# The encoder's tail in 512-token matmuls on groups of 1024 tokens, with the embeddings' product moved into the last attention units

## The chip, the cores and the metric

The kernel runs on 1 core of one Trainium2 chip. The metric is the device time of one execution in microseconds (us); the time before is the median of three runs. The engines are called by the names of the profile: PE is TensorE, DVE VectorE, ACT ScalarE, POOL GpSimd, and SP the engine whose queue issues the transfers (DMA).

## The reference

One encoder layer for two requests (prompt and sample) of 2048 tokens each, width 1024, all in float32. Two attention branches (a window of 128 tokens to both sides, and a neighbourhood on a grid of 64 columns) give 1024 columns of output per token; then come an output projection, a gate and an embeddings' product:

```python
x = x + jnp.concatenate([o_a, o_b], axis=-1) @ w_out
gate = jax.nn.sigmoid(x @ w_ple_gate)
return x + (p @ w_ple) * gate          # p: 256 columns per token
```

These three lines are the tail, and the change lies in them.

## The kernel before

**Precision.** Matmuls take two operands in a shortened float32. Each operand is split into a high part (a cast, on ACT) and the rest (a subtraction, mostly on DVE), and each product is three matmuls: high x high and the two mixed ones.

**Attention.** Blocks of 128 tokens are projected (`proj_a`, `proj_b`) and attended to in units (`unit_a`, `unit_b`). TensorE's order is written out by hand. A stream of "filler" matmuls (L943) is drawn from while a unit runs: each filler matmul has a price (108 for 256 tokens, 215 for 512), each unit has a budget of filler (L953: 10320 for most units of the second branch, `TAIL` for the last six, when no projection is left), and the tables PLAN_A and PLAN_B say at which part of the budget a step of the attention is put in. Weight splits wait as jobs in a list and are put in by `pump` and `flush`. The attention's outputs go to DRAM, those of the second branch in an order of their own (by columns of the grid).

**The tail.** Everything is transposed: rows are columns of the layer, and the moving operand of a matmul is a tile of tokens. `TW` is 256 here, so there are 16 tiles of tokens.

- `out_ahead` (L866) computes the output projection of one tile in the plain way: 8 row blocks x 8 x 3 matmuls of 256 tokens, the residual added by DVE (L882), the result x1 stored to DRAM. Three tiles (`AHEAD - 1`) are filler of the last six attention units, a fourth stands behind them. `load_o`, `split_o` and `load_ev` bring and split what it needs.
- All other products of the output projection and of the gate are made by seven products instead of eight (a scheme of Strassen's kind): the weight is cut into four blocks of 512 x 512, two tiles of 256 tokens with the two halves of the columns make four operand blocks, and sums of weight blocks (made ahead, in DRAM, `sums`) meet sums of operand blocks. A group is 512 tokens: six groups for the output projection (stage 0), eight for the gate (stage 1), seven steps each, 48 matmuls of 256 tokens a step (`product`, L1074).
- `prep` (L1039) makes the operand of a step two steps ahead: the sum in a tile of its own (POOL and DVE), the cast (ACT, L1068), the subtraction (DVE or POOL, L1053), each over 1024 elements a row.
- `result` (L1103) takes a product out of PSUM. In stage 0 the residual is added and x1 stored. In stage 1 a result is finished by an addition (L1124), tanh on ACT (L1128), a multiplication with the embeddings' product, which stands in PSUM (L1129), and the addition of x1 out of the operand's tile (L1131), then stored to the output (L1134).
- The embeddings' product (`ple_of`, L1150) is computed in stage 1, six matmuls of 256 tokens a block, between the products.

In the tail, DVE, ACT, POOL and SP are partly ordered by a scheduler, partly as written: what is wrapped in `P` or `pin` is kept in the order of the program.

Of the kernel before, what the change touches and what calls it, by code (L numbers as in the profile page):

```python
# [69 lines left out]
SB = 5  # L70
# [8 lines left out]
TAIL = 9300  # L79
HOLD = {"wa": 20, "wb": 12, "wp": 0}  # L80
TW = 256
NU = SEQ // TW
AHEAD = 4
# [15 lines left out]
def emit(ctx, tc, io):  # L99
# [706 lines left out]
    o_st, o_rs = {}, {}  # L806

    def fproj(ps, w, m, xs, nk, mm_):
        for k in range(nk):
            if mm_ is mm:  # L810
                flush(f"o{k // 4}")
                flush(("wa", "wb")[m // 4] + str(KT - 1))
            for i, (a, b) in enumerate(((0, 0), (1, 0), (0, 1))):
                mm_(ps, w[m // 4][k][:, a, 128 * (m % 4):128 * (m % 4) + 128], xs(k, b),
                    start=(k == 0 and i == 0), stop=(k == nk - 1 and i == 2))
                yield 108

    def load_o(n, tail):
        if n < len(tiles):
            s, u = tiles[n]  # L820
            o_st[n] = []
            for i in range(2):
                st = main.tile([128, 2, TW], F32, tag="stage", name="oa", bufs=2)
                nc.sync.dma_start(st, oa_d[s].rearrange("(i j p) t -> i p j t", p=128, j=2)[i, :, :, TW * u:TW * u + TW])
                o_st[n].append(st)
            for i in range(2):
                if tail:
                    st = ap.tile([128, 2, 4, 64], F32, tag="sq", name="ob", bufs=2)
                else:
                    st = main.tile([128, 2, 4, 64], F32, tag="s", name="ob", bufs=SB)  # L830
                nc.sync.dma_start(st.rearrange("p j c t -> p (j c) t"),
                                  ob_d[s][u // 2].rearrange("p (i j) c t -> i p (j c) t", i=2)
                                  [i, :, :, 64 * (u % 2):64 * (u % 2) + 64])
                o_st[n].append(st)

    def split_o(n, i):

        t = main.tile([128, 2, 2, 2, TW], F32R, tag="xr", name="o_r", bufs=2)
        st = o_st[n][2 * i:2 * i + 2]

        def job(dst, src):
            nc.scalar.copy(dst[0], src)
            nc.vector.tensor_tensor(out=dst[1], in0=src, in1=dst[0].bitcast(F32), op=ALU.subtract)
        for j in range(2):
            if i == 0:
                jobs.append((f"o{i}", partial(job, [t[:, j, a] for a in range(2)], st[j])))
            else:
                for k in range(2):
                    jobs.append((f"o{i}", partial(job, [t[:, j, a, k].rearrange("p (r k c) -> p k r c", k=4, c=16)
                                                        for a in range(2)],  # L850
                                                  st[j][:, k].rearrange("p k (r c) -> p k r c", c=16))))
        o_rs.setdefault(n, []).append(t)

    def o_hi_lo(n):
        return lambda k, b: o_rs[n][k // 4][:, k % 4 // 2, b, k % 2, :]

    def load_ev(n, mp):

        if n < AHEAD - 1:
            ev = ap.tile([128, 2, TW], F32, tag="ev", name="ev", bufs=2)  # L860
        else:
            ev = main.tile([128, 2, TW], F32, tag="s", name="ev", bufs=SB)
        nc.sync.dma_start(ev, io["x_r"][n][:, 2 * mp:2 * mp + 2])
        return ev

    def out_ahead(n, evs=None):  # L866

        tail = n < AHEAD - 1
        if n > 0:
            split_o(n, 0)  # L870
            split_o(n, 1)
        if n != AHEAD - 2:
            load_o(n + 1, tail)
        for mp in range(4):
            ps = ptile([128, 2, TW], "pj", "pout")
            for kk in range(2):
                for i, c in enumerate(fproj(ps[:, kk, :], w_b[2], 2 * mp + kk, o_hi_lo(n), KT, mm)):
                    if tail and i % 5 == 4:
                        pump()
                    yield c  # L880
            ev = evs[mp] if evs else load_ev(n, mp)
            P(nc.vector.tensor_tensor(out=ev, in0=ps, in1=ev, op=ALU.add))  # L882
            nc.sync.dma_start(x1_d[n][:, 2 * mp:2 * mp + 2], ev)
# [41 lines left out]
    def paired(f, n):  # L925

        a, b = filler(f), filler(f + 1)
        half, w = (f - 2 * NT) // (2 * NT) + 1, []
        src, c0 = (w_in_c, 1024 * half) if half < 2 else (w_out_c, 0)
        yield from islice(a, n)  # L930
        yield from islice(b, n)
        w.append(load_w(main, "wa", src, c0, KT, half < 2))
        yield from a
        if half == 2:
            load_o(0, True)
            split_o(0, 0)
        yield from b
        if half == 2:
            split_o(0, 1)
        w.append(load_w(main, "wb", src, c0 + 512, KT, half < 2))  # L940
# [38 lines left out]
    with tc.tile_pool(name="c", bufs=1) as op:  # L979

        STEPS = ("a11", "a12", "s2", "s1", "s3", "a22", "s4")
        SLOT = {"s2": 0, "s3": 1, "s4": 2, "s1": 3}

        def load_q(i, name):

            out = []
            for j in range(4):
# [5 lines left out]
                tag = {"a11": f"wa{j}", "a12": f"wa{4 + j}", "s4": f"wb{j}", "a22": f"wb{4 + j}"}.get(name, f"{name}{j}")  # L993
# [3 lines left out]
                nc.sync.dma_start(raw, src)  # L997
                jobs.append((f"{i}{name}", partial(split_w, w, raw, None, tc.keep_in_program_order)))
                out.append(w)
            return out  # L1000

        ws = [{}, {}]
        w_p = []

        raws, opds = {}, {}
        groups = [(0, g) for g in range(AHEAD // 2, NU)] + [(1, g) for g in range(NU)]

        def raw_tile(name):
            return op.tile([128, 8, TW], F32, tag="raw", name=name, bufs=4)

        def load_raw(n):
# [4 lines left out]
            if stage == 0:  # L1016
                s, b = divmod(g, 4)
                oa, ob = raw_tile("oar"), raw_tile("obr")
                oav = oa.rearrange("p a t -> p (a t)").rearrange("p (k t) -> p k t", k=4)
                obv = ob.rearrange("p a t -> p (a t)").rearrange("p (k c t) -> p k c t", k=4, c=4)  # L1020
                nc.sync.dma_start(oav, oa_d[s].rearrange("(k p) t -> p k t", p=128)[:, :, 512 * b:512 * b + 512])
                nc.sync.dma_start(ob.rearrange("p a t -> p (a t)"), ob_d[s][b].rearrange("p j c t -> p (j c t)"))
                raws[n] = [oav[:, :, :TW], oav[:, :, TW:]] + [
                    [obv[:, k].rearrange("p c (r x) -> p r c x", x=16)[:, 4 * h:4 * h + 4] for k in range(4)] for h in range(2)]
            else:
                t = [raw_tile("x1r") for _ in range(2)]
                for h in range(2):
# [75 lines left out]
        def result(n, q, mp, ps, part):  # L1103
# [16 lines left out]
            if part == 0:  # L1120
                return
# [161 lines left out]
```

## Time and profile before

| | us |
|---|---|
| runs, median (lowest, highest) of 3 | 2585.34 (2582.66, 2585.56) |
| span of the profiled execution | 2584.1 |
| PE busy in it | 2531.9 (98%) |
| DVE busy | 1922.3 (74%) |
| ACT busy | 1392.3 (54%) |
| POOL busy | 792.2 (31%) |

The profiled execution's own time is its span; it lies inside the range of the runs. How to read the rows: in rows of groups, a row names the line, the engine, the operation, what it writes and reads, the shapes and the count, then the busy time and the mean length of one in ns, then the idle time of the engine just before and what ended it. In rows of the order of time come the start, the length and how many instructions were merged; a bracket gives the idle time before and what ended it. A matmul's length is longer than its spacing, since matmuls overlap: the spacing is read from starts. The granted clock is the share of full speed that TensorE was given.

### The profile page before, as it was taken

The numbers are of one execution on the slowest core, as the hardware profiler recorded it, in microseconds if no ns is written. First come the engines' busy times: TensorE is split into PE (matmuls) and PEld (weight loads), VectorE is DVE, ScalarE is ACT, GpSimd is POOL, SyncE is SP. The second block draws the span as 40 slices with busy tenths as digits, with TensorE's granted clock in tenths as the row PEclk, the third lists the DMA queues.
The fourth block names the chain that finished last, engine by engine and source line by source line (L and its number), as shares of the span: only waits on it lengthen the run. The fifth ranks groups of instructions, "written<-read, shape, count | busy, mean of one in ns | idle before, by whom it ended". The sixth has DMA issues, their size and how long they took to land.

```text
span 2584.1 us, 47172 instructions
## 1 busy us (share of the span) xinstructions
PE 2531.9 (98%) x16080; PEld 2268.0 (88%) x16080; DVE 1922.3 (74%) x5704; ACT 1392.3 (54%) x3327; POOL 792.2 (31%) x995
## 2 busy tenths in 40 slices
PE   8999999999989999999899999999999999999999
PEld 7888888888877888888788888887999999999999
DVE  7888888888886877887878777878665648555454
ACT  6666666666664666666666666666432214223222
POOL 3333323333223333333233333321132324233321
PEclk9999999999999999999999999999999999999999
DMA  6323342111243565555665555557584455232221
GB/s 203 107 90 109 107 102 81 55 60 58 60 119 123 171 196 150 183 184 170 211 187 155 184 173 154 155 153 216 167 280 167 153 172 182 85 121 85 79 82 46
DMA packets 227551, 357.51 MB, mean 138 GB/s; under 512 B 37968, under 2 KB 115408, under 8 KB 222160
## 3 DMA queue, kind: packets, MB, share of 16 engines
q1 hardware_dynamic: 227312, 354.51, 43.8%
q8 instruction: 128, 2.10, 0.3%
q14 instruction: 111, 0.91, 0.1%
HBM read 266.33 MB, written 105.92 MB: 144 GB/s over the span
## 4 chain that ended last, share of the span: by engine, by line
PE 85%; DVE 8%; ACT 3%; issue 2%; DMA 2%; POOL 1%; SPq 0%; DVEq 0%; ACTq 0%; POOLq 0%
PE pqk L212 12%; PE pvg L212 12%; PE acca L1087 11%; PE accc L1087 8%; PE pq L212 6%; PE pg L212 6%; PE pple L212 4%; PE pout L212 3%; PE ptb L215 3%; PE pk L212 3%; PE scb L212 3%; PE pob L212 3%; PE sc L212 3%; PE po L212 3%; PE pt L215 3%
## 5 line engine op out<-in xcount | busy, mean ns | idle before, releaser
L243 ACT ACTIVATE s<-s,nm 128x384 f32<-128x384 f32 (+4 forms) x512 | 307.2, 601 | 360.3 <-DVE nm L238 232.3
L212 PE MATMUL pvg<-wb,xr 128*128 128x512 f32 x1536 | 460.4, 407 | 0.0
L212 PE MATMUL pqk<-wa,xr 128*128 128x512 f32 x1536 | 444.0, 411 | 0.0
L308 POOL TENSOR_TENSOR xr<-stx,xr 128x512 fp32r<-128x512 f32 x190 | 245.1, 1298 | 186.7 <-ACT xr L307 179.4
L212 PEld LDWEIGHTS pqk<-wa,xr 128*128 128x128 f32 x1536 | 267.4, 190 | 37.7
L212 PEld LDWEIGHTS pvg<-wb,xr 128*128 128x128 f32 x1536 | 267.2, 189 | 31.1
L212 PE MATMUL pg<-wb,xr 128*128 128x512 f32 x768 | 232.6, 410 | 0.0
L212 PE MATMUL pq<-wa,xr 128*128 128x512 f32 x768 | 221.2, 402 | 2.8 <-DVE wa L160 2.8
L798 POOL TENSOR_TENSOR o_tb<-otb 128x256 f32<-128x256 f32 x64 | 48.9, 763 | 559.4 <-DVE otb L791 469.8
L1087 PE MATMUL acca<-opd,s 128*128 128x256 f32 x1344 | 164.7, 283 | 3.6 <-ACT r L1119 2.5
L1087 PEld LDWEIGHTS acca<-opd,s 128*128 128x128 f32 x1344 | 162.6, 192 | 4.4 <-ACT r L1119 2.7
L212 PEld LDWEIGHTS pq<-wa,xr 128*128 128x128 f32 x768 | 140.1, 190 | 26.4 <-DVE wa L160 3.8
L227 DVE CUSTOM_DVE_ANT_0 s<-scb,bias 128x288 f32<-128x288 f32 (+3 forms) x256 | 141.5, 553 | 21.0 <-PE scb L212 18.5
L212 PEld LDWEIGHTS pg<-wb,xr 128*128 128x128 f32 x768 | 138.0, 190 | 20.5
L212 PEld LDWEIGHTS pob<-p_t,vw 128*128 128x128 f32 (+2 forms) x832 | 131.7, 190 | 24.9 <-DVE q L719 3.7
L646 DVE SCALAR_TENSOR_TENSOR ks_b<-pktb,wk,ks_b 64x128 fp32r<-64x128 f32 x256 | 115.1, 450 | 44.1 <-ACT ks_b L645 33.8
L1053 POOL TENSOR_TENSOR opd<-sum,opd 128x1024 fp32r<-128x1024 f32 x28 | 69.8, 2494 | 233.6 <-ACT opd L1068 233.6
L645 ACT ACTIVATE ks_b<-pktb,wk 64x128 fp32r<-64x128 f32 x256 | 124.6, 487 | 30.7 <-DVE ks_b L646 24.5
L772 DVE TENSOR_TENSOR p_t<-ptb,p_t 128x368 fp32r<-128x368 f32 (+5 forms) x256 | 125.2, 490 | 18.4 <-ACT p_t L771 11.1
L215 PE MATMUL ptb<-rowwise,s 128*128 128x128 f32 (+2 forms) x832 | 133.4, 274 | 3.7 <-ACT s L243 3.7
L605 DVE TENSOR_TENSOR pr<-pt,pr 128x512 fp32r<-128x512 f32 x184 | 125.3, 684 | 14.9 <-ACT pr L604 13.9
L227 DVE CUSTOM_DVE_ANT_0 s<-sc,mask 128x384 f32<-128x384 f32 (+1 forms) x256 | 132.6, 537 | 3.1 <-PE sc L212 0.7
(201 smaller groups left out, 5846.2 us busy)
## 6 DMA issues: line engine op xcount, KB each, us to landing
stx<-x_b SPq DMA_DIRECT2D x128, 256.0 KB
vw<-v_d SPq DMA_DIRECT2D x112, 256.0 KB
stx<-x_a SPq DMA_DIRECT2D x64, 256.0 KB
stn<-x_n SPq DMA_DIRECT2D x64, 256.0 KB
v_d<-vb SPq DMA_DIRECT2D x64, 256.0 KB
x1r<-x_d SPq DMA_DIRECT2D x16, 1024.0 KB
y_t<-r SPq DMA_DIRECT2D x64, 256.0 KB
v_d<-vb SPq DMA_DIRECT2D x96, 128.0 KB
```

What stands on the lines that cost most here:

```text
L212: pinned(nc.tensor.matmul(out, lhsT, rhs, start=start, stop=stop))
L215: pinned(nc.tensor.transpose(out, in_, eye))
L227: nc.vector.tensor_tensor_reduce(out=s[:, :n], in0=ps[:, :n], in1=bias, scale=1.0, scalar=-3.0e38, op0=ALU.add, op1=ALU.max, accum_out=sm[ ...
L243: ex = nc.scalar.activation(ss[i][:, :n], ss[i][:, :n], AF.Exp, bias=nm[:, i:i + 1], accum_out=den[:, i:i + 1])
L308: low.tensor_tensor(out=lo, in0=raw, in1=hi.bitcast(F32), op=ALU.subtract)
L605: nc.vector.tensor_tensor(out=pr[:, 1], in0=pf, in1=pr[:, 0].bitcast(F32), op=ALU.subtract)
L645: nc.scalar.activation(hi, pkt[a:a + 64, i], AF.Copy, scale=wk[a:a + 64, 1:2])
L646: nc.vector.scalar_tensor_tensor(out=lo, in0=pkt[a:a + 64, i], scalar=wk[a:a + 64, 1:2], in1=hi.bitcast(F32), op0=ALU.mult, op1=ALU.subtract)
L772: nc.vector.tensor_tensor(out=lo, in0=pf, in1=hi.bitcast(F32), op=ALU.subtract)
L798: nc.gpsimd.tensor_tensor(out=o_t, in0=got["ot"][:, :, 0], in1=got["ot"][:, :, 1], op=ALU.add)
L1053: each(lambda x, y, z: pin(eng.tensor_tensor(out=x, in0=y, in1=z, op=ALU.subtract)), out, a, b)
L1087: pinned(nc.tensor.matmul(ps[:, kk], w[k][:, a, c:c + 128], o[:, b, k], start=i in (0, 1, 4) and kk == 0 and k == 0 and j == 0, stop=k == ...
```

## The change

`TW` becomes 512, so there are 8 tiles of tokens, and a group of the split products is 1024 tokens: four groups for the output projection and four for the gate, 7 steps of 48 matmuls of 512 tokens each. No tile is projected in the plain way any more.

The embeddings' product is computed ahead for all tiles (`ple_ahead`): tiles 0 to 4 (`AHEAD` is 5) are the filler of the last six attention units, whose budget falls from 9300 to 8600; tiles 5 to 7 stand behind them. ACT copies each block out of PSUM, and it is stored to DRAM (`ple_d`). In the gate it is loaded again block by block, and so is x1 for the residual (`load_x`: eight tiles in flight, two loads for each result).

Sums of operand blocks are formed in place in the loaded tiles (`combos`, on POOL and once on DVE), one step or more ahead; five operand tiles of 8 KB a row are in use. A step's operand is split in four pieces (`piece`) during the step before it. A result is one block of 128 rows x 512 tokens. The accumulators keep the four blocks of one chain in four banks of PSUM. All of this is wrapped in `P`, so that DVE, ACT, POOL and SP work in the order of the program. The weights of the first steps are loaded and split during the embeddings' product (`load_early`).

```diff
-TAIL = 9300
+TAIL = 8600
-TW = 256
+TW = 512
-AHEAD = 4
+AHEAD = 5
...
+    def split_p(n, later=False):
+        t = p_rs[n] = main.tile([128, 2, 2, TW], F32R, tag="xr", name="p_r", bufs=2)
+        def job(hi, lo, src):
+            nc.scalar.copy(hi, src)
+            nc.vector.tensor_tensor(out=lo, in0=src, in1=hi.bitcast(F32), op=ALU.subtract)
...
+    def ple_ahead(n, tail=False):
+        load_p(n + 1)
+        for m in range(KT):
+            ps = ptile([128, TW], "pj", "pple")
+            if m == 5 and n + 1 < len(tiles):
+                split_p(n + 1)
+            flush("p")
+            flush("p0")
+            for k in range(2):
+                w, c = early["p"][2 * (m // 4) + k], 128 * (m % 4)
+                for i, (a, b) in enumerate(((0, 0), (0, 1), (1, 0))):
+                    mm(ps, w[:, a, c:c + 128], p_rs[n][:, k, b], k == 0 and i == 0, k == 1 and i == 2)
+                    yield 215
+            if n > 0 or m > 5:
+                pump()
+            if tail:
+                ev = main.tile([128, TW], F32, tag="s", name="ev", bufs=SB)
             else:
+                ev = ap.tile([128, TW], F32, tag="ev", name="ev", bufs=2)
+            P(nc.scalar.copy(ev, ps))
+            nc.sync.dma_start(ple_d[n][:, m], ev)
...
-                   *(out_ahead(n) for n in range(AHEAD - 1)))
+                   *(ple_ahead(n) for n in range(AHEAD)))
...
-    with tc.tile_pool(name="c", bufs=1) as op:
+    with tc.tile_pool(name="c", bufs=1, reuse_waits="tile") as op:
...
+        def combos(n, i, k):
+            if i == 0:
+                if k == 0:
+                    raws[n, 4] = op.tile([128, 4, TW], F32, tag="raw", name="raw", bufs=5), False
+                less(nc.vector, n, k, 0, 2, 0)
+                less(nc.gpsimd, n, k, 4, 3, 0)
+            elif i == 2:
+                less(nc.gpsimd, n, k, 2, 3, 2)
+            elif i == 3:
+                less(nc.gpsimd, n, k, 4, 1, 4)
...
+        def piece(m, k):
...
+            P(nc.scalar.copy(hi, v))
+            P(nc.vector.tensor_tensor(out=lo, in0=v, in1=hi.bitcast(F32), op=ALU.subtract))
...
+        def product(m, mi):
...
+            for k in range(4):
+                o = opds[m, k]
+                for j, (a, b) in enumerate(((0, 0), (1, 0), (0, 1))):
+                    pinned(nc.tensor.matmul(ps, w[k][:, a, c:c + 128], o[:, b], start=i in (0, 1, 4) and k == 0 and j == 0,
+                                            stop=k == 3 and j == 2, skip_group_check=True))
...
         def load_x():
             if to_load:
+                x = main.tile([128, TW], F32, tag="stage", name="xres", bufs=2) if count[0] % 8 < 2 else \
+                    op.tile([128, TW], F32, tag="xres", name="xres", bufs=6)
+                P(nc.sync.dma_start(x, to_load.pop(0)))
...
+            P(nc.scalar.activation(r, ps if first else r, AF.Tanh, scale=0.5))
+            P(V.scalar_tensor_tensor(out=r, in0=r, scalar=1.0, in1=loaded.pop(0), op0=ALU.add, op1=ALU.mult))
+            P(V.scalar_tensor_tensor(out=r, in0=r, scalar=0.5, in1=loaded.pop(0), op0=ALU.mult, op1=ALU.add))
             load_x()
+            load_x()
...
+        load_raw(0, 0)
+        drain(ple_ahead(AHEAD, True))
+        load_raw(0, 1)
+        drain(ple_ahead(AHEAD + 1, True))
...
         for m in range(7 * len(groups)):
             n, i = divmod(m, 7)
+            if i >= 3:
+                load_raw(n + 1, i - 3)
...
+            for mi in range(4):
+                combos(n, i, mi)
+                for k in range(2 * mi, 2 * mi + 2) if mi < 2 else ():
+                    piece(m + 1, k)
+                result(n, i, mi, product(m, mi))
```

More of the change, by code (lines that the diff above doesn't have):

```diff
@@ L818, in load_o, with load_p @@
-    def load_o(n, tail):
+    ple_d = [dram.tile([128, KT, TW], F32, tag=f"ple_d{n}", name=f"ple_d{n}") for n in range(len(tiles))]
+    p_st, p_rs, early = {}, {}, {}
+    def load_p(n):
         if n < len(tiles):
             s, u = tiles[n]
[L821 to L828, printed above, removed]
-                else:
[L830 to L834, printed above, removed]
@@ L854, in o_hi_lo @@
[L854 to L883, printed above, removed]
+            p_st[n] = []
@@ new lines, in emit, with result @@
+        res = {}
+        def result(n, i, mi, ps):
+            stage, g = groups[n]
+            h, t = ((0, 0), (0, 0), (1, 0), (1, 1), (1, 1), (1, 0), (0, 1))[i]
+            first, final = i not in (1, 4, 5), i not in (0, 2, 3)
+            V = nc.vector
+            if first:
+                r = main.tile([128, TW], F32, tag="s", name="r", bufs=SB) if count[1] % 9 < SB else \
+                    op.tile([128, TW], F32, tag="r", name="r", bufs=9 - SB)
+                count[1] += 1
+                if stage == 0:
+                    P(V.tensor_tensor(out=r, in0=ps, in1=loaded.pop(0), op=ALU.add))
+                    load_x()
+                elif not final:
+                    P(nc.scalar.copy(r, ps))
+                res[h, t, mi] = r
+            if not final:
```

318 lines of the change are left out of this document (124 added, 194 removed).

## The prediction

> **What bounds the kernel now.** I read the page first, then stretches of the span with each engine's busy time, then TensorE's order of time, then single groups and queues.
>
> ```profile
> span 2584.1 us, 47172 instructions
> PE 2531.9 (98%) x16080; PEld 2268.0 (88%) x16080; DVE 1922.3 (74%) x5704; ACT 1392.3 (54%) x3327; POOL 792.2 (31%) x995
> ...
> PE 85%; DVE 8%; ACT 3%; issue 2%; DMA 2%; POOL 1%; SPq 0%; DVEq 0%; ACTq 0%; POOLq 0%
> ```
>
> TensorE is busy 98% of the span and carries 85% of the chain that ended last. A change pays if it takes TensorE time away; what it does to the other engines matters only where TensorE would then wait. The diff touches nothing before the last six attention units; each engine's order is the same up to there. So I read the stretches from 1778 us on (start:end, length, busy time and count of each engine, granted clock, DMA share, GB/s).
>
> ```profile
> 1778.00:1792.00 14.00, 9.11 (x57) 8.27 (x56) 12.53 (x28) 10.81 (x29) 1.88 (x3) 0.76 0.85 242
> 1792.00:1890.00 98.00, 97.08 (x804) 96.31 (x803) 61.21 (x157) 45.81 (x119) 13.17 (x23) 1.00 0.60 178
> 1890.00:1910.00 20.00, 20.00 (x169) 20.00 (x168) 5.93 (x8) 4.71 (x9) 2.84 (x4) 1.00 0.92 309
> 1910.00:1950.00 40.00, 35.61 (x282) 35.26 (x282) 34.52 (x42) 12.76 (x22) 17.28 (x11) 0.96 0.83 286
> 2160.00:2200.00 40.00, 37.49 (x312) 37.28 (x311) 35.01 (x37) 17.33 (x28) 15.47 (x6) 1.00 0.29 102
> 2200.00:2550.00 350.00, 350.00 (x2919) 350.00 (x2918) 185.57 (x224) 102.04 (x142) 102.84 (x46) 1.00 0.27 87
> ```
>
> From 2200 to 2550 us TensorE never waits: 350/2919 = 119.9 ns per 256-token matmul. There only the cost of a matmul can be improved. Waits lie at the start of the last attention units (1778), the start of the split products (1910) and the change to the gate (2160). The marks in TensorE's order of time:
>
> ```profile
> 1778.57 0.48 PE L212 MATMUL pout<-o_r,wa 128*128 128x256 f32 x2
> ...
> 1782.76 0.51 PE L212 MATMUL pout<-o_r,wa 128*128 128x256 f32 x2 [1.65 <-ACT o_r L842]
> 1786.29 0.79 PE L212 MATMUL pout<-o_r,wa 128*128 128x256 f32 x2 [3.02 <-DVE o_r L843]
> ...
> 1898.54 11.68 PE L212 MATMUL pout<-o_r,wb 128*128 128x256 f32 x96
> 1910.06 5.92 PE L1087 MATMUL acca<-opd,wa 128*128 128x256 f32 x48
> ...
> 2184.19 6.02 PE L1087 MATMUL acca<-opd,s 128*128 128x256 f32 x48 [2.51 <-ACT r L1119]
> ...
> 2575.97 3.04 PE L1087 MATMUL acca<-opd,wb 128*128 128x256 f32 x24
> ```
>
> The reader sees three sections: 131.5 us from the first output-projection matmul (1778.57) to the first split product (1910.06); 668.8 us from there to the end of the last matmul (2575.97 + 24 x 0.12 = 2578.85); 5.3 us to the end of the span.
>
> **The price of a 512-token matmul.** The tail has none today; the projections have. Runs without another group inside:
>
> ```profile
> 35.74 3.34 PE L212 MATMUL pg<-wb,xr 128*128 128x512 f32 x14
> 38.92 0.27 PE L215 MATMUL pkt<-ident,kt 128*128 128x128 f32 x1
> ...
> 1765.30 2.27 PE L212 MATMUL pvg<-wb,xr 128*128 128x512 f32 x9
> 1767.41 0.40 PE L212 MATMUL scb<-ks_b,q1b 128*128 128x512 f32 x1
> ...
> 1808.14 2.36 PE L212 MATMUL pout<-o_r,wb 128*128 128x256 f32 x18
> 1810.34 0.32 PE L212 MATMUL scb<-ks_b,q1b 128*128 128x360 f32 x1
> ```
>
> (38.92 - 35.74)/14 = 227 ns in a quiet stretch; (1767.41 - 1765.30)/9 = 234 ns right behind a 256-token group in busy attention. A 256-token matmul within attention costs (1810.34 - 1808.14)/18 = 122 ns. Two of the tail's cost 239.8. I take 227.5 ns for the tail, because its 256-token matmuls already run as undisturbed as that quiet stretch, and 232 within attention.
>
> [...]
>
> **The change, part by part.**
>
> *Counts.* Before, from 1778.57 on: 768 plain output-projection matmuls (4 tiles), 4704 of split products (14 groups x 336), 768 of the embeddings' product; 6240 in all, of 256 tokens. After: 384 for the embeddings (8 tiles x 48), 2688 for the products (8 groups x 7 x 48); 3072 in all, of 512 tokens. The columns fall too, 6240 to 6144, since no tile is left plain.
>
> *First section, 131.5 us.* Out go 768 matmuls: 576 in attention at 122 ns and 192 at (1910.06 - 1898.54)/96 = 120 ns, 93.3 us. In come 384: 240 in the six units (40 each, by the budget of 8600 at 215) at 232 ns and 144 behind them at 227.5, 88.4 us. -4.9. The attention work between them stays. The waits at 1782 and 1786 (4.7 us) and the half clock behind them (0.76 over 14 us: 3.4) came from splitting both halves of the attention's output and eight weight tiles just in time; the embeddings' product needs two input tiles and, to begin, two weight tiles. -8. New waits: the second weight tile's split now stands on ACT behind four exponentials, where one stood at 1779.44, about 1.5 us after it is wanted. And each result goes by a copy on ACT (as long as the copies out of PSUM in the tail) through one of two buffers to DRAM; of SP's issues the load behind a store waits for its end:
>
> ```profile
> 1779.44 1.65 ACT L163 CAST wa<-wa 128x512 fp32r<-128x512 f32 x3
> ...
> L1119 ACT COPY r<-acca 128x512 f32<-128x512 f32 x48 | 28.1, 587 | 81.8 <-PE acca L1087 81.8
> ...
> 1870.51 0.32 SPq L883 DMA_DIRECT2D x_d<-ev  x1
> 1872.89 0.33 SPq L863 DMA_DIRECT2D ev<-x_r  x1
> ...
> SPq L743 <- PE pob L212: 222.0, 46, 7.2
> ```
>
> The store took 2.4 us, with ACT's copy of 0.59 3 us for a buffer, so two serve one result per 1.5 us; one comes per 83/40 = 2.1 us. The 40 copies are 23.5 us more for an ACT that was busy 45.81 of 98 us here, so its time suffices. SP, however, also stops up to 7.2 us at loads of values that wait for TensorE, with the stores queued behind; then ACT stops at its next copy, and the exponentials with it. Bound 0 to 10 us, taken 3: mostly covered, as the three PSUM buffers hold 4 us. Section: 131.5 - 4.9 - 8 + 1.5 + 3 = 123.1.
>
> *Second section, 668.8 us.* 2688 x 227.5 = 611.5 us of matmuls in place of 5472 x 119.9 = 656.1 and 12.7 of waits. What may wait now:
>
> The sums are formed in place on POOL (12 per group, half the size of these) and DVE, and everything on DVE stands in the order written. The gate's result is a chain there (columns as above, then neighbours with the idle time before them):
>
> ```profile
> 2401.93 0.69 DVE L1124 TENSOR_TENSOR r<-accc,r 128x512 f32<-128x512 f32 x1 [1.53 <-PE accc L1087]
> 2403.32 0.69 DVE L1129 SCALAR_TENSOR_TENSOR r<-r,pple 128x512 f32<-128x512 f32 x1 [0.70 <-ACT r L1128]
> 2404.05 0.69 DVE L1131 SCALAR_TENSOR_TENSOR r<-r,x1r 128x512 f32<-128x512 f32 x1
> ...
> L164 DVE TENSOR_TENSOR wb<-wb 128x512 fp32r<-128x512 f32 x12 | 7.5, 684 | 0.0
> L1053 POOL TENSOR_TENSOR sum<-x1r 128x1024 f32<-128x1024 f32 x24 | 61.2, 2552 | 25.7 <-DVE opd L1053 24.4
> ...
> 2162.17 6.90 DVE L164 TENSOR_TENSOR s<-s 128x512 fp32r<-128x512 f32 x4
> ```
>
> One result takes 2404.05 + 0.69 - 2401.93 = 2.81 us, tanh included, and nothing fills the 0.70 any more. A step lasts 48 x 0.2275 = 10.9 us and has four results and four splits of 0.68 for the next: 4 x 2.81 + 2.7 = 14.0 us in steps 2, 5 and 6, 4 x 1.4 + 2.7 = 8.4 in step 7 (no add), about 5.5, 2.7 and 2.7 in the others: 61 of 76.4 us per group. Steps 5 to 7 in a row need 36.4 against 32.8, so DVE falls behind by about 8 us, but the splits stand ahead of the last three results, and by this count they are ready 0 to 2 us before TensorE wants them. Splits also stop while POOL works: four of them took 6.9 us at 2162 instead of 4 x 0.68. Taken 4 us over the four gate groups, bound 0 to 20 (a wait of 1.3 us at each of four places per group).
>
> SP issues 52 transfers per gate group (32 loads for the results, 16 stores, 4 operands) where it issued 24; at the 0.32 and 0.33 us of the rows above that is 17 of 76.4 us. Traffic per gate group is 4 MB for the operands, 8 of embeddings and residual, 4 of result: 16.8e6 bytes / 76.4 us = 220 GB/s, and in steps 5 to 7 up to 384, above the 309 at share 0.92; loads are issued four results (over 11 us) ahead. At zero; without that cover it is the last rival. At the start three tiles of the embeddings (33 us) cover the loads of the four operands and of the sums' weights, which now need no output of the plain tiles; taken 2 us, bound 0 to 8. Section 611.5 + 6 = 617.5, -51.3.
>
> *End.* ACT and DVE finish as before; DVE is 3 us behind, of which 0.5 shows. 5.8.
>
> *Sum.* 1778.6 + 123.1 + 617.5 + 5.8 = 2525.0 us of span, 59 less. The median of the runs is 2585.34, 1.2 over this span: 2526.
>
> **The rivals.**
>
> *A, the 512-token matmul is spaced at nearly twice the 256-token one*, between the 234 of busy attention and the 239.8 of two. For it: that 234. Against: the 227. 2832 x 6.5 to 12.3 ns and 240 x 2 to 7.8 are 19 to 37 us more: 2545 to 2563, 2554 in the middle. [...]
>
> *B, DVE's fixed order becomes the bound of the gate.* If POOL or a semaphore lengthens a result from 2.81 to 3.3 us, eight results in a row bring 4 us per group and the splits are late at the steps 2, 7 and 1: with the bound above 16 to 20 us, 2544. For it: the 36.4 against 32.8. Against: light steps 1, 3 and 4.
>
> *C, the round trip of the embeddings stops the gate*: slower than before. Each of the 64 gate results stands on DVE behind two loads. DVE has 15 us to spare per group, 0.9 us per result; the gain is 59/64 = 0.9 us per result. So from about 1.9 us of wait at every result the kernel is slower. Price at 2.2 us: 2526 + 64 x 1.3 = 2609. For it: three transfers per result in one queue, with the bursts above 309 GB/s. Against: 220 on the mean, and loads 11 us ahead.
>
> *D, the last attention units stall*: SP's stops are as long at each unit, 6 x 2.5 = 15 us more, 2541.
>
> **How the numbers follow.** My forecast (2526, own range 2511 to 2541) 0.60; A 0.10; B 0.13; D 0.07; C 0.07; faster than the range 0.03. The low end is no new wait (-10.5), 1 ns less per matmul (-3) and 227 in attention (-1): 2511. The range goes down to 2506, as the runs shown of one kernel lie 2.9 us apart, and up into A: 2506 to 2556 leaves out C, the 0.03, the upper half of A and what adds up of B and D. Faster by over 0.2% (5 us, about what a measurement of this kernel can tell from no change): all but C and 0.01 beside it, 0.92; same 0.01; slower 0.07.
>
> **What would show it.** In the profile after: starts of gate matmuls 227 ns apart, a stretch of 300 us in the tail with about 1320 of them and TensorE busy throughout; the first product of the split section near 1901 us instead of 1910; no half clock near 1785; waits of TensorE on DVE's splits at most 1 us each. I am wrong if the spacing is 235 or more, if ACT's copies of the embeddings wait for stores by microseconds, or if DVE waits for loads in the gate's results.

## The result and the profile after

| | before | after |
|---|---|---|
| runs, median (lowest, highest) | 2584.70 (2582.66, 2585.56) of 4 | 2553.25 (2549.44, 2554.36) of 4 |
| ratio to before, with 95% interval | 1 | 0.9876 [0.9862, 0.9890] |
| span of the profiled execution | 2584.1 | 2547.2 |

The change gains 31 us where 59 were forecast (2526). The page of the changed kernel: its span, the busy times, and the chain that ended last.

```profile
span 2547.2 us, 41396 instructions
...
PE 2486.1 (98%) x12912; PEld 2091.2 (82%) x12912; DVE 1946.9 (76%) x5764; ACT 1443.8 (57%) x3469; POOL 733.2 (29%) x969
...
PE 83%; DVE 8%; DMA 3%; ACT 3%; issue 2%; POOL 0%; SPq 0%; ACTq 0%; DVEq 0%; POOLq 0%
```

PE's busy time fell by 45.8 us, the span by 36.9: some of the gain went into waits. Where they lie is seen in stretches of the changed kernel (columns as in the prediction):

```profile
1778.00:1792.00 14.00, 12.37 (x65) 9.76 (x64) 11.39 (x27) 10.32 (x21) 0.40 (x1) 1.00 0.97 299
1792.00:1870.00 78.00, 73.35 (x398) 59.20 (x397) 47.77 (x124) 59.02 (x141) 13.08 (x21) 1.00 0.70 228
1900.00:1915.00 15.00, 4.84 (x21) 3.70 (x20) 3.29 (x6) 4.43 (x9) 0.00 (x0) 0.80 0.85 317
1915.00:1950.00 35.00, 35.00 (x147) 28.82 (x146) 24.45 (x34) 13.87 (x26) 16.98 (x12) 0.94 0.66 226
2160.00:2200.00 40.00, 40.00 (x178) 33.15 (x177) 27.11 (x35) 9.87 (x17) 15.37 (x10) 1.00 0.71 238
2225.00:2260.00 35.00, 32.19 (x135) 26.15 (x134) 28.37 (x35) 13.21 (x25) 21.49 (x12) 0.95 0.43 137
2260.00:2540.00 280.00, 275.96 (x1208) 225.47 (x1206) 206.19 (x278) 113.73 (x209) 58.18 (x36) 1.00 0.62 205
```

At 2160, where TensorE used to wait, it runs through. The waits now lie among the last attention units (73.35 of 78), at 1900 to 1915 (4.84 of 15, with half clock from within the wait on), at the start of the gate (32.19 of 35) and, thinly, through the gate. TensorE's order of time gives the marks:

```profile
1774.92 0.48 PE L212 MATMUL pple<-p_r,wa 128*128 128x512 f32 x1
...
1874.03 30.21 PE L212 MATMUL pple<-p_r,wa 128*128 128x512 f32 x132
1914.40 5.19 PE L212 MATMUL pple<-p_r,wa 128*128 128x512 f32 x12 [10.16 <-ACT ev L870]
1919.42 5.84 PE L1082 MATMUL acca<-opd,wa 128*128 128x512 f32 x25
...
2246.08 4.61 PE L1082 MATMUL accc<-opd,wb 128*128 128x512 f32 x12 [2.81 <-DVE r L1126]
...
2528.18 11.04 PE L1082 MATMUL acca<-opd,wa 128*128 128x512 f32 x48
```

These marks cut the span into parts that can be set beside the forecast, whose first section of 123.1 us is 90.3 in attention and 144 x 0.2275 = 32.8 behind it. "Start" is the first embeddings' matmul, "attention" runs to the last attention matmul, "last tiles" to the first split product, "products" to the end of the last matmul, "end" to the end of the span. All in us; the last two columns are the median of the runs and the ratio to the kernel before, run on the same chip.

| kernel | start | attention | last tiles | products | end | span | median | ratio |
|---|---|---|---|---|---|---|---|---|
| forecast | 1778.6 | 90.3 | 32.8 | 617.5 | 5.8 | 2525.0 | 2526 | |
| after | 1774.9 | 99.1 | 45.4 | 619.6 | 8.2 | 2547.2 | 2553.25 | 0.9876 |
| after, again | 1776.0 | 101.0 | 44.9 | 620.0 | 9.1 | 2551.0 | 2553.80 | 0.9865 [0.9850, 0.9880] |
| s2 behind | 1779.0 | 101.6 | 35.2 | 626.4 | 9.0 | 2551.2 | 2550.51 | 0.9862 [0.9848, 0.9877] |
| s2 not split | 1778.0 | 103.4 | 34.0 | 627.8 | 8.5 | 2551.8 | 2551.57 | 0.9861 [0.9845, 0.9878] |
| halves | 1778.5 | 102.0 | 44.9 | 648.9 | 6.5 | 2580.8 | 2582.82 | 0.9984 [0.9973, 0.9995] |
| three buffers | 1777.0 | 94.8 | 45.2 | 619.3 | 8.8 | 2545.2 | 2546.80 | 0.9850 [0.9836, 0.9865] |
| stores by POOL | 1775.3 | 105.7 | 45.9 | 619.3 | 8.2 | 2554.3 | 2557.29 | 0.9887 [0.9873, 0.9900] |
| s2 early | 1775.2 | 102.3 | 35.7 | 619.7 | 9.6 | 2542.5 | 2542.54 | 0.9828 [0.9814, 0.9841] |
| gate spread | 1777.0 | 99.2 | 44.8 | 616.0 | 8.2 | 2545.2 | 2547.65 | 0.9852 [0.9838, 0.9865] |
| no add | 1777.6 | 99.1 | 44.7 | 614.0 | 5.0 | 2540.4 | 2541.79 | 0.9822 [0.9806, 0.9839] |
| no filling | 1777.8 | 67.2 | 105.4 | 620.2 | 8.2 | 2578.9 | 2580.66 | 0.9973 [0.9962, 0.9984] |
| three edits | 1775.7 | 95.3 | 36.8 | 615.9 | 8.1 | 2531.8 | 2533.70 | 0.9793 [0.9779, 0.9806] |
| three edits, s2 earlier still | 1776.8 | 95.1 | 36.2 | 616.6 | 9.3 | 2533.9 | 2534.70 | 0.9793 [0.9778, 0.9808] |

The row "after" against the forecast: -3.7 + 8.8 + 12.6 + 2.1 + 2.4 = 22.2 us. The start lies in work that no edit touches; it differs by up to 4 us among these profiles of the changed code, so the -3.7 is not put down to the change. The profiled execution is also the quickest of its four, 3.8 below their median.

### The profile page after: what moved, and what is told of

It reads as the page before. It is cut to its first block, busy times and chain, and to the rows that moved or that the text cites. A ratio compares the mean times of both kernels' runs of the same rounds, so it can differ in the third digit from the quotient of the medians.

```text
span 2547.2 us, 41396 instructions
## 1 busy us (share of the span) xinstructions
PE 2486.1 (98%) x12912; PEld 2091.2 (82%) x12912; DVE 1946.9 (76%) x5764; ACT 1443.8 (57%) x3469; POOL 733.2 (29%) x969
## 4 chain that ended last, share of the span: by engine, by line
PE 83%; DVE 8%; DMA 3%; ACT 3%; issue 2%; POOL 0%; SPq 0%; ACTq 0%; DVEq 0%; POOLq 0%
PE pqk L212 13%; PE pvg L212 13%; PE acca L1082 11%; PE accc L1082 8%; PE pq L212 6%; PE pg L212 6%; PE scb L212 3%; PE ptb L215 3%; PE pk L212 3%; PE pob L212 3%; PE sc L212 3%; PE po L212 3%; PE pt L215 3%; PE pple L212 2%; DMA ple_d<-ev 1%
## 5 line engine op out<-in xcount | busy, mean ns | idle before, releaser
L1028 POOL TENSOR_TENSOR raw<-raw 128x512 f32<-128x512 f32 x96 | 152.3, 1614 | 460.7 <-DVE raw L1028 284.8
L1064 ACT CAST opd<-raw 128x512 fp32r<-128x512 f32 x224 | 130.4, 620 | 256.6 <-PE acca L1082 105.5
L1065 DVE TENSOR_TENSOR opd<-raw,opd 128x512 fp32r<-128x512 f32 x224 | 183.1, 853 | 120.0 <-ACT opd L1064 120.0
L1082 PE MATMUL accc<-opd,wb 128*128 128x512 f32 x768 | 178.6, 392 | 2.8 <-DVE r L1126 2.8
L1082 PE MATMUL acca<-opd,s 128*128 128x512 f32 x768 | 177.5, 390 | 2.8 <-ACT r L1120 2.4
L1082 PE MATMUL acca<-opd,wa 128*128 128x512 f32 x768 | 175.9, 389 | 0.5 <-DVE opd L1065 0.5
L1082 PEld LDWEIGHTS accc<-opd,wb 128*128 128x128 f32 x768 | 145.2, 189 | 33.5 <-DVE r L1126 3.2
L1082 PEld LDWEIGHTS acca<-opd,s 128*128 128x128 f32 x768 | 143.5, 188 | 35.5 <-ACT r L1120 4.0
L1082 PEld LDWEIGHTS acca<-opd,wa 128*128 128x128 f32 x768 | 144.1, 188 | 30.8 <-DVE opd L1065 0.9
L212 PEld LDWEIGHTS pg<-wb,xr 128*128 128x128 f32 x768 | 138.0, 190 | 20.6
```

Of the source, the lines that this page charges most:

```text
L212: pinned(nc.tensor.matmul(out, lhsT, rhs, start=start, stop=stop))
L1028: each(lambda x, y, z: eng.tensor_tensor(out=x, in0=y, in1=z, op=ALU.subtract), k, *(raws[n, i] for i in (out, a, b)))
L1064: P(nc.scalar.copy(hi, v))
L1065: P(nc.vector.tensor_tensor(out=lo, in0=v, in1=hi.bitcast(F32), op=ALU.subtract))
L1082: pinned(nc.tensor.matmul(ps, w[k][:, a, c:c + 128], o[:, b], start=i in (0, 1, 4) and k == 0 and j == 0, stop=k == 3 and j == 2, skip_gro ...
```

## The experiments

**What the joining is worth.** The first question was whether the forecast's main term, 512-token matmuls spaced well under two of 256, is real. In the split products every matmul was issued as two halves:

```diff
-    pinned(nc.tensor.matmul(ps, w[k][:, a, c:c + 128], o[:, b], ...))
+    for z in (slice(0, 256), slice(256, 512)):
+        pinned(nc.tensor.matmul(ps[:, z], w[k][:, a, c:c + 128], o[:, b, z], ...))
```

> The changed kernel with each of the 2688 512-token matmuls of the split products issued as two of 256 tokens on the halves of the same PSUM tile. It measures what the joining alone is worth. By the spacings of the two traces (226.8 ns against two of 119.9 ns): 2688 x 13.0 ns = 35 us more, 2588, that is slower than the kernel before by 0.1%, less up to 10 us if TensorE's waits in the gate are covered by the longer steps: 2578 to 2590. [...]

Each half of a PSUM tile is begun by a start of its own here, and the output is not the layer's; the number and size of the matmuls are as said. Measured: 2582.82 us, 29 more than the changed kernel, so nearly all of its gain is gone. A stretch of this kernel:

```profile
2050.00:2150.00 100.00, 100.00 (x836) 100.00 (x835) 51.94 (x74) 20.52 (x35) 17.26 (x12) 1.00 0.49 162
```

100/836 = 119.6 ns here, against 40/178 = 225 ns for the changed kernel at 2160 (over all split products, by starts without waits: 120.1 and 226.8). A joined pair saves 13.4 ns, 36 us over 2688; 7 of them come back because the slower stream waits less in the gate. Rival A falls. From the two spacings, an estimate: 13.4 ns for each matmul with its weight load, and (226.8 - 120.1)/256 = 0.417 ns for each token. Joining two matmuls joins their two weight loads as well, and weight loads are busy 100.00 of 100 us here against 33.15 of 40 in the changed kernel; which of the two carries the 13.4 ns is not shown.

**The 10 us at 1914.** TensorE waited for ACT's copies of the embeddings (L870). ACT's and SP's order of time in the changed kernel, in two fences:

```profile
1900.72 2.18 ACT L1064 CAST opd<-raw 128x512 fp32r<-128x512 f32 x4
1913.24 0.62 ACT L163 CAST s<-s 128x512 fp32r<-128x512 f32 x1 [10.34 <-DMA s<-sums]
1913.76 0.58 ACT L870 COPY ev<-pple 128x512 f32<-128x512 f32 x1
```

```profile
1899.30 0.43 SPq L1014 DMA_DIRECT2D raw<-oa_d  x1
1899.78 1.08 SPq L1016 DMA_DIRECT2D raw<-ob_d  x1
1900.95 1.61 SPq L871 DMA_DIRECT2D ple_d<-ev  x3
1902.62 5.95 SPq L996 DMA_DIRECT2D s<-sums  x4
```

The load of the summed weights s2 (`load_q(0, "s2")`, L1151) stands in the middle of the last embeddings' tile. It puts four split jobs on the list, and the `pump` inside `ple_ahead` draws one of them for each block from there on, ahead of the block's copy. ACT came to the first cast at 1902.9; its data was being asked for from 1902.62 on, behind two loads of 1 MB. So ACT stood for 10.34 us before a cast whose weights are used in the third step, two steps of 10.9 us after the first product; the copies stood behind it, no PSUM tile came free, and TensorE stood as well. Two edits tell the place of the casts from the place of the load: the load moved behind the tile, or the load left and the pump taken out of that tile.

```diff
-        load_q(0, "s2")
         drain(rest)
+        load_q(0, "s2")
```

> The changed kernel with the load of the weights s2 issued behind the last tile of the embeddings' product instead of in its middle. Theory O (order on ACT): the four casts of s2 stood on ACT between the copies of the last tile and waited 10.34 us for their load, so TensorE waited 10.16 us for its PSUM tiles and then ran at half clock (12 matmuls in 5.2 us instead of 2.7). Without them the first split product starts at about 1906.5 us instead of 1919.4, TensorE's wait of 10 us is gone, and the time falls by 12 to 13 us from 2553.25 to about 2540.5 (2538 to 2543). Rival T (traffic): the transfers of that stretch (0.9 of the queues' time busy, two loads of 1 MB, stores, residual tiles) are what is late; then the wait appears at the next load, on the operands or on s2 in front of the second step, and the time stays above 2549.

```diff
-            if n > 0 or m > 5:
+            if (n > 0 or m > 5) and n + 1 < len(tiles):
                 pump()
```

> The changed kernel with the load of s2 where it is, but without the split jobs drawn between the blocks of the last embeddings' tile: the splits of s2 come at the flush of the second step. It tells the order of the casts on ACT apart from the place of the load. Theory O: as with the later load, 2540.5 (2538 to 2543), the first split product at about 1906.5 us. Theory T, or the place of the load on SP's queue (its four issues took 5.95 us with two stores of the embeddings behind): no gain or less than half of it, 2547 to 2553.

Measured: 2550.51 and 2551.57. The two agree, so it is the casts' place on ACT and not the load's place in SP's queue. The wait at 1914 went in both (last tiles 35.2 and 34.0). But the time fell by 2 to 3 us only, and "after, again" lies at 2553.80 with an interval that overlaps: theory O was right about the wait and wrong about the gain. The products grew by 7 to 8 us. TensorE, DVE and POOL of the kernel with s2 behind:

```profile
1939.77 4.61 PE L1082 MATMUL accc<-opd,wb 128*128 128x512 f32 x12 [4.80 <-DVE r L1126]
...
1930.37 6.48 DVE L164 TENSOR_TENSOR s<-s 128x512 fp32r<-128x512 f32 x4
...
1929.92 8.04 POOL L1028 TENSOR_TENSOR raw<-raw 128x512 f32<-128x512 f32 x5 [0.63 <-DMA xres<-x_r]
```

Drawn later, the four subtractions meet POOL's sums and take 6.48 us instead of 4 x 0.68; the results stand behind them on DVE, and the accumulators are not freed. The early splitting had been hiding this. That asks for a third place: split early, load earlier still.

```diff
         load_raw(0, 1)
+        load_q(0, "s2")
         drain(ple_ahead(AHEAD + 1, True))
...
-        load_q(0, "s2")
         drain(rest)
...
-            if n > 0 or m > 5:
+            if (n > 0 or m > 5) and n != len(tiles) - 2:
```

> The changed kernel with the load of s2 issued one embeddings' tile earlier, ahead of the two loads of 1 MB, and its splits drawn in the first half of the last tile, 12 us behind the load. The later load (2550.51) took the 10 us wait at 1914 away but TensorE then waited 4.9 us at 1940 for DVE, where the four splits stood beside POOL's sums. Theory O2 (the splits are wanted before the sums begin, and only the load was late): no wait over 1 us from 1875 to 2231, the section from the first embeddings' matmul to the first split product at 130 to 134 us instead of 144.5, the one behind it at 617 to 620, and 2540.5 (2538 to 2543). Rival T (the transfers of the stretch are what is late): a wait of 5 us or more at another load or store there, above 2547.

Measured: 2542.54, 11 us less than the changed kernel, and no wait in the products up to 2231. TensorE's order there:

```profile
1889.80 11.04 PE L212 MATMUL pple<-p_r,wa 128*128 128x512 f32 x48
1902.17 11.24 PE L212 MATMUL pple<-p_r,wa 128*128 128x512 f32 x48 [1.32 <-ACT ev L870]
1913.24 3.11 PE L1082 MATMUL acca<-opd,wa 128*128 128x512 f32 x13
```

The section up to the first product is 138.0 us, not the 130 to 134 expected: this run's attention part was long (102.3), and a remnant stays, since ACT waited 4.1 us for a store behind the s2 loads and TensorE 1.32. So traffic has a share, a small one; the order is the main cause.

**The attention part, 99 us against 90.3.** ACT's and the weight loads' waits there in the changed kernel (engine, line, waited for; us in total, times, longest):

```profile
ACT ev L870 <- DMA ple_d<-ev: 13.3, 12, 2.8
...
PEld pple L212 <- ACT ev L870: 5.9, 9, 2.1
```

ACT finds both buffers still being stored. Too few buffers, or stores held up in SP's queue? One edit gives a third buffer, the other issues the stores from POOL's queue with two:

```diff
-                ev = ap.tile([128, TW], F32, tag="ev", name="ev", bufs=2)
+                ev = ap.tile([128, TW], F32, tag="ev", name="ev", bufs=3)
```

> The changed kernel with three instead of two buffers for the embeddings' copies during the last attention units. In the trace ACT waited there 13.3 us in 12 waits for the stores out of these buffers, and TensorE some 6 us for PSUM tiles behind the copies. Theory B (two buffers are too few): ACT's waits for stores fall below 5 us, and the time falls by 3 to 6 us, 2547 to 2550. Rival Q (SP's queue: each store is issued late behind loads that wait): a third buffer moves the wait by one result only; 2551 to 2554, ACT's waits for stores stay above 8 us.

```diff
-            nc.sync.dma_start(ple_d[n][:, m], ev)
+            (nc.sync if tail else nc.gpsimd).dma_start(ple_d[n][:, m], ev)
```

> The changed kernel with the stores of the embeddings' results during the last attention units issued from POOL's queue instead of SP's, two buffers as before. It tells SP's stops apart from the number of buffers as the cause of ACT's waits for stores (14.7 us between 1774 and 1925 in the trace of the changed kernel, 20 to 25 us in three runs with the same attention code). If the stores stand behind SP's other issues (its loads of values that wait for TensorE, its result stores that wait for DVE): ACT's waits for stores below 8 us, the attention part (first embeddings' matmul to last attention matmul, 99 to 102 us) shorter by 4 us or more. If the round of copy, issue and store is too long for two buffers by itself: waits and the part as before, or longer, since POOL's own work of some 10 to 15 us lies in front of stores.

Three buffers: 2546.80, attention 94.8. Stores by POOL: 2557.29, attention 105.7. The waits of the first, then of the second:

```profile
PEld pple L212 <- ACT ev L870: 2.5, 4, 1.0
ACT ev L870 <- DMA ple_d<-ev: 2.2, 1, 2.2
```

```profile
ACT ev L870 <- DMA ple_d<-ev: 18.2, 18, 3.5
...
POOL ple_d L871 <- ACT ev L870: 37.0, 19, 3.8
```

Out of SP's queue the stores are waited for no less (18.2 us against 13.3), and POOL now stops 37 us for ACT's copies with its own attention work behind it. Alone, this does not clear SP, since POOL's own work now stands in front of the stores. The trace of the changed kernel does: of the 40 stores, 30 are issued within 0.1 us of the end of their copy, and the latest 1.8 us behind it. One round in ACT's and SP's order of time; the two copies share a buffer:

```profile
1810.03 0.57 ACT L870 COPY ev<-pple 128x512 f32<-128x512 f32 x1
...
1810.63 0.34 SPq L871 DMA_DIRECT2D ple_d<-ev  x1
...
1815.63 0.59 ACT L870 COPY ev<-pple 128x512 f32<-128x512 f32 x1 [1.16 <-DMA ple_d<-ev]
```

The store was issued at once and held the buffer for 5.0 us. Over the 13 waits of more than 0.1 us, it was 2.1 to 5.6 us from the issue of the store to the next copy, 3.8 in the mean, where the prediction had read 2.4. So the round of copy and store is too long for two buffers by itself; theory B holds, and SP's stops, the price that rival D gave, are at most a small part.

**What the filling is worth.** A budget of 1 puts the same five tiles behind the units.

```diff
-TAIL = 8600
+TAIL = 1
```

> The changed kernel with the same five tiles of the embeddings' product put behind the last attention units instead of between their instructions (the budget of a unit set to 1). It measures what the filling is worth. The six units issue about 44 us of matmuls of their own by their spacings; the filled part took 99 to 102 us with 240 x 0.232 = 56 us of filling. If the units alone are bound by their chains of softmax on ACT and DVE, they take 60 to 80 us without filling, so that the filling hides 16 to 36 us and the time rises to 2570 to 2590. If the filled units cost as much as the two one after the other (the fill is hidden by nothing), the time stays within 5 us of 2553.

Measured: 2580.66. Bare, the six units take 67.2 us, and TensorE is busy in 52.48 of 70:

```profile
1775.00:1845.00 70.00, 52.48 (x300) 43.22 (x299) 50.82 (x143) 47.07 (x124) 14.68 (x26) 0.91 0.59 178
```

The last-tiles part grows by 60; 67.2 + 60.3 less the 99 to 101 of the filled part is 26 to 28 us hidden, which is the difference of the medians (27). Without it little is left of the change's gain, 7 us.

**The gate.** The first gate group's wait of 2.81 us at 2246 looks like the one that s2 made. DVE there in the changed kernel:

```profile
2236.29 6.86 DVE L164 TENSOR_TENSOR s<-s 128x512 fp32r<-128x512 f32 x4 [3.70 <-ACT s L163]
2243.08 2.35 DVE L1065 TENSOR_TENSOR opd<-raw,opd 128x512 fp32r<-128x512 f32 x2
2245.35 0.68 DVE L1126 TENSOR_TENSOR r<-accc,r 128x512 f32<-128x512 f32 x1
```

Four splits in a row, beside POOL's sums, ahead of the first result of the step. One edit spreads the twelve splits of the first gate group over two steps that finish no results:

```diff
                 result(n, i, mi, product(m, mi))
+                if n == n_o and i in (2, 3):
+                    pump(2 - mi % 2)
...
-            elif n == n_o and i < 3:
-                flush("1" + STEPS[i + 4])
```

> The changed kernel with the last twelve splits of the gate's weights, which stood in blocks of four at the start of steps 2, 3 and 4 of the first gate group, spread one or two behind each result over steps 3 and 4. Theory S (four splits in a row beside POOL's sums hold up DVE's results): TensorE's wait of 2.95 us at 2246 and the half clock behind it go, and one of 1.6 us near 2262 in some runs; the part from the first split product to the last matmul falls from 619.6 to about 615, the time by 4 us to 2549. Rival (DVE's chain of results itself is too long, rival B of the prediction): the wait stays or comes back within the same group, 2552 to 2555.

Measured: 2547.65, products 616.0 (-3.6). The stretch at the start of the gate, 32.19 busy before, is now

```profile
2225.00:2260.00 35.00, 34.85 (x154) 28.39 (x153) 28.37 (x35) 13.61 (x26) 21.59 (x12) 1.00 0.48 151
```

and the half clock behind the wait is gone too. The second edit leaves out the last VectorE operation of a gate result (L1132, half the product plus the residual, which the output then lacks), to price DVE's chain.

```diff
-            P(V.scalar_tensor_tensor(out=r, in0=r, scalar=0.5, in1=loaded.pop(0), op0=ALU.mult, op1=ALU.add))
+            loaded.pop(0)
```

> The changed kernel without the last VectorE operation of each gate result (half the product plus the residual); it leaves the residual out, so its output is not the reference's; all loads and everything else stay. It prices DVE's chain of results (rival B of the prediction): 64 x 0.69 us less on DVE. If that chain is behind TensorE's waits in the gate (1.6 us at 2418, some of 0.5 to 0.8) and behind the end (8.2 us from the last matmul's end to the end of the span, forecast 5.8): the end falls to 5.5 to 6.5, the waits of the gate but the one at 2246 go, together 5 to 7 us less, 2547. If POOL's sums beside DVE are behind both: end and waits stay, 2552 to 2554.

Measured: 2541.79, 12 us less than the changed kernel on the same chip, where 5 to 7 were expected; 6 of them in the products, 4 at the end. TensorE's waits in the gate of the changed kernel, then of this one:

```profile
PE accc L1082 <- DVE r L1126: 2.8, 1, 2.8
PE acca L1082 <- ACT r L1120: 2.4, 3, 1.4
PE acca L1082 <- DVE opd L1065: 0.8, 2, 0.5
```

```profile
PE accc L1082 <- DVE r L1126: 2.8, 1, 2.8
```

What is left is the wait at the splits. And the end in DVE's order, the changed kernel, then this one:

```profile
2540.90 0.68 DVE L1131 SCALAR_TENSOR_TENSOR r<-r,xres 128x512 f32<-128x512 f32 x1
2541.62 0.69 DVE L1132 SCALAR_TENSOR_TENSOR r<-r,xres 128x512 f32<-128x512 f32 x1
2542.23 0.68 DVE L1131 SCALAR_TENSOR_TENSOR r<-r,xres 128x512 f32<-128x512 f32 x1
2542.95 0.69 DVE L1132 SCALAR_TENSOR_TENSOR r<-r,xres 128x512 f32<-128x512 f32 x1
```

```profile
2533.51 0.69 DVE L1131 SCALAR_TENSOR_TENSOR r<-r,xres 128x512 f32<-128x512 f32 x1 [2.03 <-ACT r L1130]
2536.23 0.69 DVE L1131 SCALAR_TENSOR_TENSOR r<-r,xres 128x512 f32<-128x512 f32 x1 [2.03 <-ACT r L1130]
```

In the changed kernel DVE works its last results off without a pause, until 2543.6, 4.6 us behind the last matmul (2539.1). With one operation less it pauses 2 us for each result, for the tanh that waits for TensorE.

**The edits together.**

> The three edits together: three buffers for the embeddings' copies, s2 loaded one tile earlier, the gate's last twelve splits spread. If the causes are separate their gains add: 6 of the buffers, 12.5 of s2, 4 of the gate, 2553 - 22.5 = 2531 (2527 to 2536). If one queue is behind all of them, the waits move on and it stays above 2540.

Measured: 2533.70, ratio 0.9793 [0.9779, 0.9806], 20 us below the changed kernel, where the gains measured one by one (6.5, 10.7 and 5.6) add up to 22.8; these medians come from several chips, and by the ratios to the kernel before, against the mean of the changed kernel's two, it is 20 us and a sum of 21. From 1950 to 2230 TensorE never waits, and the gate is nearly closed:

```profile
1950.00:2230.00 280.00, 280.00 (x1237) 231.86 (x1236) 171.26 (x240) 73.51 (x129) 68.70 (x43) 1.00 0.58 191
2230.00:2260.00 30.00, 29.20 (x128) 23.20 (x127) 25.07 (x33) 17.05 (x33) 8.51 (x6) 1.00 0.54 176
```

One wait of 2.1 us was left at 1895, behind a store that stood behind the s2 loads. Moving these one tile earlier still, with no pump in the two tiles before the last:

```diff
-            if (n > 0 or m > 5) and n != len(tiles) - 2:
+            if (n > 0 or m > 5) and not AHEAD <= n < len(tiles) - 1:
                 pump()
...
         load_raw(0, 0)
+        load_q(0, "s2")
         drain(ple_ahead(AHEAD, True))
         load_raw(0, 1)
-        load_q(0, "s2")
```

> The three edits of the combination with the loads of s2 one tile earlier still, behind the first load of 1 MB. In the combination ACT waited 4.9 us for a store at 1890 and TensorE 2.2 us, behind the s2 loads in the same queue. If the crowd of transfers at 1884 is the cause, that wait goes: 2531 (2529 to 2534). If any load of s2 in front of the stores costs the same, it comes back at about 1880: 2533 to 2536.

Measured: 2534.70, no change. The wait moved to 1888 and shrank to 1.2 us. In both kernels four more transfers stand in front of the stores, and their times agree (2533.70 and 2534.70).

**The changed kernel once more.**

> The changed kernel itself once more, on the chip of these runs, as the measure for the edits: 2553 (2549 to 2556); it also shows how far its attention part, 99.1 us in the first profile against 101.6 to 103.4 in three runs with the same code there, varies by itself.

Measured: 2553.80 (2549.54 to 2554.82), attention 101.0. In the eight profiles whose edits do not touch that part (all but three buffers, stores by POOL, no filling and the combinations) it lies between 99.1 and 103.4, so a single profile cannot settle a difference of 2 us there; the 94.8 to 95.3 of the three kernels with a third buffer lie below all eight.

## Why the prediction was right and wrong

**Right: the matmuls.** Forecast 227.5 ns in the tail, measured 226.8; 13.4 ns saved per pair against 12.3. The products' matmuls took 2688 x 0.2268 = 609.6 us, 1.9 under the forecast. Marks that it named for them also came: from 1930 to 2230 TensorE is busy 300.00 of 300 us with 1326 matmuls, and there is no half clock at 1785.

**Wrong: the first section, +21 us.** The first product came at 1919, not near 1901. Two steps failed.

- "At the start three tiles of the embeddings (33 us) cover the loads of the four operands and of the sums' weights": the 33 us are there, but the cover was counted for TensorE's need of s2, in the third step. I overlooked that the pump inside the embeddings' product draws the casts of s2 as soon as they are on the list. ACT, in fixed order, then waits 10.34 us at a cast that stands ahead of the copies which TensorE needs next. Price: 12.6 us with the half clock around it, against the 2 (0 to 8) that were taken.
- "Bound 0 to 10 us, taken 3: mostly covered, as the three PSUM buffers hold 4 us": mis-sized. The 1.5 us of service per result rested on a store of 2.4 us. Where ACT waited, the store took 3.8 us in the mean; with the copy that is 4.7 us for a buffer, and two buffers then serve one result per 2.3 us, no faster than the one per 2.1 us that was to come. Results also come in bunches, because the filler runs between two steps of a unit in one piece, and ACT waited for stores 12 times, up to 2.8 us. The part came out 8.8 us longer, within the bound of that term together with rival D's 15. The third buffer takes 4 to 6 of it back. The remaining 5 were not followed up by an edit; with three buffers TensorE is still idle for 5.6 of the 94.8 us, 3.2 of them for DVE's attention work.

"ACT's copies of the embeddings wait for stores by microseconds" stood in the prediction as a sign that it is wrong, and so it was.

**Nearly right: the gate, +2, and the end, +2.4.** Four us of waits were taken over the gate groups (bound 0 to 20), and about 10 came, 1.7 of them as half clock; the matmuls' 1.9 and the 2 us not spent at the start hide that in the sum. The mechanism was the one named: DVE's fixed order, 36.4 us of work against 32.8 in steps 5 to 7, and splits slowed beside POOL. Its own terms make DVE's lag 2 x (14.0 - 10.9) = 6.2 us, not the 8 that it states. Two sizes were off besides. "The splits stand ahead of the last three results, and by this count they are ready 0 to 2 us before TensorE wants them" left out that four splits of weights stand in DVE's order at the start of the second step, and that operations with two inputs in SBUF took longer here beside POOL: at 2246.73, while POOL formed a sum, a result's multiplication took 1.62 us, at 2248.38, with POOL idle, its addition 0.69. And "DVE is 3 us behind, of which 0.5 shows" at the end: 2.9 showed. Rival B, priced at 16 to 20 us, thus holds in kind for the 6 us of the products that went with the last operation of a result; the other 4 stand at the splits of the weights, which it did not name.

**Rivals C and D.** C falls: in the gate DVE never waits for a load of the round trip through DRAM; its waits there are for ACT, and 1.2 us for TensorE. D's symptom came, but by the buffers and not by SP's stops. That the range held the time is luck for the most part: it had been opened towards slower times for rivals A, B and D, and the time lies there because of the casts of s2, which no rival named, and of the length of the stores, where D had named SP's stops.

## What to carry to other kernels

Where an engine's order is fixed, look for every place that can put an instruction into it, and ask of each when its data lands and what stands behind it: a cast that was wanted two steps later cost 12 us, and moving it back met a second collision that its early place had avoided. The mean rate of a buffer's round says little when results come in bunches; a third buffer of 2 KB a row was worth 6 us. A change that pays by its matmuls is worth a second look at the other engines' order: three edits of a few lines gained 20 us more than the 31.

## What was not expected of the hardware

- While POOL formed sums, operations of VectorE with two inputs in SBUF took longer here. The four splits at 2236 took 6.86 us (1.7 each, against 0.68), and POOL's sums took 1.7 us there, against 1.28 where they run alone. An addition with one input in PSUM took 0.68 us beside the same sums (2245.35). It goes the other way too: POOL's sum at 2228.60 took 5.15 us while VectorE ran such operations without a pause at 0.68 each. What makes the two engines hold each other up is not shown.
- Half clock came in steps: around the wait of 10 us TensorE's granted clock was 0.50 for 10.24 us (from 1908.85 on), behind that of 2.81 us for 3.41 (from 2246.77 on), around the waits at 1782 and 1786 of the kernel before for 6.83 (from 1783.73 on), all multiples of 3.41. Whether a wait came with half clock depended on more than its length: in the kernel with s2 behind TensorE was idle for as long, 2.81 of the 8 us from 2244 to 2252, and the clock stayed at 1.00 from 2240 to 2260. In the changed kernel TensorE was busy for 0.69 of the last 3.41 us before the half clock, in the other for 2.30 and 2.89 us of the two halves of those 8. What decides it is not shown.
